# The values' projection of a fused encoder layer: one quarter of k goes from eight block products to seven

## The chip, the cores and the metric

The kernel runs on one core of one Trainium2 chip. The metric is the device time of one execution in microseconds (us), lower is better. The kernel before takes 1814.43 us (median of 3 runs, 1814.18 to 1815.42). Engines are called as the profile calls them: PE is TensorE (matmul), ACT is ScalarE, DVE is VectorE, POOL is GpSimd, SP is SyncE; SP and POOL here mainly issue DMAs. PSUM, where matmuls accumulate, has eight banks of 128 x 512 f32 on this kernel's count.

## The reference, cut to what matters

One layer of a streaming encoder on 256 tokens of width 2048. Of it, the change touches the input projection, and of that only the last 1024 columns, the values of the attention:

```python
h = rms_norm(x, mix_norm[i])
proj = h @ w_in[i]                  # (256 x 2048) @ (2048 x 4096)
u = proj[..., :SSM_WIDTH]           # 1024 columns; then q, k and v, 1024 each
v = proj[..., SSM_WIDTH + 2 * SB_WIDTH:].reshape(bsz, seq, SB_HEADS, SB_HEAD_DIM)
y_ssm = s5_mixer(u, ...)            # ends in a gate: z * sigmoid(z @ w_glu + b_glu)
y_sb = stick_breaking_attention(q, k, v.transpose(0, 2, 1, 3))
```

## The kernel before, in words

**Products in three parts.** All big products are taken in fp32r, in three parts: a weight piece of 256 rows by 512 columns (128 x 1024 in SBUF) is split into a rounded part `whi` (ACT, a CAST at line 182) and the rest `wlo` (DVE, a subtraction at line 185); the activations are split once into `nhi` and `nlo`. A product is hi x hi, hi x lo and lo x hi, summed in PSUM. Lines 341 and 346 are those matmuls in a plain block, lines 530, 531 and 533 in a group of seven (below). Each matmul is 128 x 128 against 128 x 512.

**A plain block** (`gemm_block`) takes 512 columns of a weight matrix. It goes over k in quarters of 512 rows (called kb 0 to 3; one DMA of 1 MB each, into a tile `raw`), each in two halves of 256 rows. A half is 12 matmuls: two token tiles of 128, times two k tiles of 128, times three parts. The two token tiles have a PSUM bank each (`acc`, four banks in turn). The values are two plain blocks before, so 2 x 8 x 12 = 192 matmuls, and `values` scales each bank into the tiles `v` on ACT (line 1554).

**A group of seven** (class `Seven`, used in the feed-forward parts) takes a quarter of k of two column blocks as a 2 x 2 problem: two token tiles and two k halves on the left, two k halves (b11, b21 of the first block, b12, b22 of the second) on the right. Instead of 8 products of 6 matmuls it needs 7, for which some operands are sums: of the weights, t1 = b11 + b12, t2 = t1 + b22, t4 = t2 + b21 (DVE, line 537, in `add`) and b12 + b22 (a DMA with accumulation, issued by POOL, line 598); of the activations, four sums made by `sum_forms` (DVE, line 487) and split into `hhi` and `hlo`. Every one of the seven right operands is split by ACT and DVE. In `single`, a form of it with few banks, products 1, 6 and 7 use one bank one after the other, and ACT or DVE takes the bank's contents out in between.

**What runs beside it.** Every half of a block ends in a call of `step()`, which hands one step to whatever was put off. During the values these are: the turning and scaling of the keys' second block (`qk_turn`, line 1327, and `qk_scale`, line 1334), the attention's scores for two pairs of heads (PE, lines 1354 to 1364), their logarithms and exponentials (ACT: Abs 1372, Exp 1373, Ln 1379, each change of function with an ACT_TABLE_LOAD), the splits `sph` and `spl` of the result, the sums over keys (PE, lines 1393 to 1400), and the splits `hhi` of the gate's input (`zt`). The gate's product (`glu`, lines 1489 to 1498) follows the values directly.

**What sets the order.** Each engine works its instructions off in the order in which they stand in its list; a scheduler of the framework sets these lists when the kernel is built, from its own estimate of when things are ready, and need not keep the program's order except where the code says `pin` or `issue_after`. Weights come through the tile `raw` of 1 MB, of which five exist; two hold x during the whole middle part, so three are in turn. Whatever is loaded next waits on SP for the release of the tile three loads back. Of `whi` and of `wlo` there are four each.

Of the kernel before, what the change touches and what calls it, by code (L numbers as in the profile page):

```python
# [12 lines left out]
AF = mybir.ActivationFunctionType  # L13
# [13 lines left out]
NB = 512  # L27
# [6 lines left out]
def layer_kernel(ctx: ExitStack, tc: tile.TileContext, a: dict, shapes: dict, out: bass.AP):  # L34
# [44 lines left out]
    def acc(s="acc"):  # L79
        return accp.tile([P, NB], F32, tag="acc", name=uid(s))  # L80
# [275 lines left out]
    def gemm_block(act, w, n0, nkt, first=()):  # L356

        ps = [acc(), acc()]
        for k0 in range(0, nkt, 4):
            part = act(k0 // 4)  # L360
            quarter = first[k0 // 4] if k0 // 4 < len(first) else weight_halves(w, k0, min(4, nkt - k0), n0)
            for half in list(quarter):
                k = k0 + 2 * half[0]
                gemm_half(ps, (part, half), range(TT), k == 0, k + 2 == nkt, in_turn=first and k0 == 0)
                if first and half[0] == 0 and k0 + 4 < nkt:
                    act(k0 // 4 + 1)
                step()
        return ps
# [123 lines left out]
    class Seven:  # L492
# [28 lines left out]
            self.last = split(hi, lo, src)  # L521
            return hi, lo

        def multiply(self, z, left, parts, final):
            hi, lo = parts
            ps = self.bank(z)
            begin = self.begin(z)
            lh, ll = left
            for j in range(2):
                nc.tensor.matmul(ps, lhsT=lh[j], rhs=hi[:, j], start=begin and j == 0, stop=False)  # L530
                nc.tensor.matmul(ps, lhsT=ll[j], rhs=hi[:, j], start=False, stop=False)  # L531
            for j in range(2):
                nc.tensor.matmul(ps, lhsT=lh[j], rhs=lo[:, j], start=False, stop=z in final and j == 1)  # L533

        def add(self, x, y):
            t = self.pool.tile([P, 2, NB], F32, tag="sum", name=uid("sum"), bufs=2)
# [22 lines left out]
        def single(self, kb, one, six, seven):  # L559
# [27 lines left out]
            put_off(0, nc.vector.tensor_tensor, seven, self.bank(7), six, ALU.add)  # L587
            step()

        def chunk(self, kb, final=()):  # L590

            if ring[0] is None:
# [956 lines left out]
    put_off(16, attn_out, pool, 0, ysb, sqa)  # L1549
    vt = [get(pool, f"v{t}") for t in range(TT)]  # L1550

    def values(n, ps):
        for t in range(TT):
            pin(nc.scalar.activation(vt[t][:, n * NB : (n + 1) * NB], ps[t], AF.Copy, scale=nm.rs(t)))
# [279 lines left out]
```

## Time and profile before

| | |
|---|---|
| median of 3 runs | 1814.43 us |
| the profiled execution, its own time | 1814.06 us |
| its span in the profile | 1812.3 us |
| PE busy | 1805.9 us, 8914 matmuls |
| DVE busy | 1573.8 us |
| ACT busy | 1063.8 us |
| granted clock of PE | 1.00 |
| the values' matmuls | from 853.8 to 903.3 us |

The span is what the profile covers, the execution's own time holds 1.8 us around it. "Busy" is the time in which an engine had something in work; a chain of waits follows, from the last instruction back, what each had to wait for. In the chain a matmul's piece goes from the end of the one before to its own end. A row of the timeline gives start, duration, engine, line, operation, `output<-inputs` with shapes, a count, and in brackets the idle time before it and what ended it.

### The profile page before, as it was taken

The numbers are of one execution on the slowest core, as the hardware profiler recorded it, in microseconds if no ns is written. First come the engines' busy times: TensorE is split into PE (matmuls) and PEld (weight loads), VectorE is DVE, ScalarE is ACT, GpSimd is POOL, SyncE is SP. The second block draws the span as 40 slices with busy tenths as digits, with TensorE's granted clock in tenths as the row PEclk, the third lists the DMA queues.
The fourth block names the chain that finished last, engine by engine and source line by source line (L and its number), as shares of the span: only waits on it lengthen the run. The fifth ranks groups of instructions, "written<-read, shape, count | busy, mean of one in ns | idle before, by whom it ended". The sixth has DMA issues, their size and how long they took to land.

```text
span 1812.3 us, 24211 instructions
## 1 busy us (share of the span) xinstructions
PE 1805.9 (100%) x8914; PEld 1497.3 (83%) x8914; DVE 1573.8 (87%) x1840; ACT 1063.8 (59%) x1240; POOL 104.8 (6%) x160
## 2 busy tenths in 40 slices
PE   9999999999999999999999999999999999999998
PEld 8888888888888888888898888888888888888887
DVE  7998889999998896697567899999999999889875
ACT  7445456555565665456695566555565556567664
POOL 0020100000000001010021000000000010000000
PEclk9999999999999999999999999999999999999999
DMA  9599867787776667674646687787767786666663
GB/s 382 208 306 309 253 220 234 238 276 219 256 274 209 197 229 257 190 256 156 219 147 219 226 300 221 265 269 233 233 232 240 239 273 229 239 209 224 200 244 128
DMA packets 107799, 428.41 MB, mean 236 GB/s; under 512 B 24512, under 2 KB 48352, under 8 KB 65280
## 3 DMA queue, kind: packets, MB, share of 16 engines
q1 hardware_dynamic: 96832, 391.15, 61.2%
q0 software_dynamic: 10560, 35.40, 9.0%
q8 instruction: 70, 1.15, 0.3%
q14 instruction: 49, 0.40, 0.1%
q10 hardware_dynamic: 288, 0.31, 0.1%
HBM read 372.41 MB, written 10.88 MB: 211 GB/s over the span
## 4 chain that ended last, share of the span: by engine, by line
PE 99%; DMA 1%; DVE 0%; ACT 0%; SPq 0%; issue 0%; DVEq 0%; ACTq 0%
PE acc L346 33%; PE acc L341 16%; PE aux L346 15%; PE aux L341 7%; PE acc L530 5%; PE acc L533 5%; PE acc L531 5%; PE aux L530 3%; PE aux L533 3%; PE aux L531 3%; DMA raw<-in_ffn_w_gate 1%; PE aux L1242 0%; PE acc L1498 0%; PE acc L1493 0%; PE acc L1489 0%; PE aux L1187 0%
## 5 line engine op out<-in xcount | busy, mean ns | idle before, releaser
L185 DVE TENSOR_TENSOR wlo<-raw,whi 128x1024 fp32r<-128x1024 f32 x478 | 579.4, 1225 | 124.0 <-ACT whi L182 117.4
L182 ACT CAST whi<-raw 128x1024 fp32r<-128x1024 f32 x478 | 496.3, 1050 | 291.9 <-PE acc L346 181.6
L346 PE MATMUL acc<-whi,nhi 128*128 128x512 f32 x908 | 355.7, 392 | 0.4 <-ACT whi L182 0.4
L346 PE MATMUL acc<-whi,nlo 128*128 128x512 f32 x908 | 353.3, 390 | 0.0
L341 PE MATMUL acc<-wlo,nhi 128*128 128x512 f32 x908 | 252.8, 389 | 0.0
L185 DVE TENSOR_TENSOR slo<-raw,shi 128x1024 fp32r<-128x1024 f32 x186 | 226.8, 1219 | 14.1 <-ACT shi L182 13.8
L182 ACT CAST shi<-raw 128x1024 fp32r<-128x1024 f32 x186 | 195.2, 1050 | 59.6 <-DMA raw<-in_ffn_w_down 23.5
L346 PEld LDWEIGHTS acc<-whi,nhi 128*128 128x128 f32 x908 | 170.6, 188 | 37.0 <-ACT whi L182 0.8
L341 PEld LDWEIGHTS acc<-wlo,nhi 128*128 128x128 f32 x908 | 170.5, 188 | 35.7 <-DVE wlo L185 0.3
L346 PEld LDWEIGHTS acc<-whi,nlo 128*128 128x128 f32 x908 | 170.8, 188 | 34.8
L182 ACT CAST whi<-sum 128x1024 fp32r<-128x1024 f32 x79 | 83.2, 1054 | 161.2 <-DVE sum L537 141.0
L182 ACT CAST shi<-sum 128x1024 fp32r<-128x1024 f32 x59 | 62.1, 1053 | 105.0 <-DVE sum L537 93.3
L537 DVE TENSOR_TENSOR sum<-sum,raw 128x1024 f32<-128x1024 f32 x92 | 112.5, 1222 | 0.9
L185 DVE TENSOR_TENSOR wlo<-sum,whi 128x1024 fp32r<-128x1024 f32 x79 | 96.5, 1224 | 5.2 <-ACT whi L182 4.5
L598 POOL DMA_DIRECT2D raw<-raw x44 | 38.1, 867 | 1032.6 <-DVE sum L537 722.4
L346 PE MATMUL aux<-whi,nhi 128*128 128x512 f32 x220 | 85.7, 390 | 0.0
L346 PE MATMUL aux<-whi,nlo 128*128 128x512 f32 x220 | 85.6, 389 | 0.0
L185 DVE TENSOR_TENSOR slo<-sum,shi 128x1024 fp32r<-128x1024 f32 x59 | 72.1, 1222 | 1.1 <-ACT shi L182 0.5
L341 PE MATMUL aux<-wlo,nhi 128*128 128x512 f32 x220 | 67.7, 389 | 0.0
L537 DVE TENSOR_TENSOR sum<-raw,raw 128x1024 f32<-128x1024 f32 x46 | 56.2, 1222 | 8.0 <-DMA raw<-in_ffn_w_down 7.2
L346 PE MATMUL acc<-whi,hhi 128*128 128x512 f32 x156 | 60.7, 389 | 0.0
L346 PE MATMUL acc<-whi,hlo 128*128 128x512 f32 x156 | 60.7, 389 | 0.0
(392 smaller groups left out, 3402.6 us busy)
## 6 DMA issues: line engine op xcount, KB each, us to landing
raw<-in_ffn_w_up SPq DMA_DIRECT2D x88, 1024.0 KB, 5.6
raw<-in_ffn_w_down SPq DMA_DIRECT2D x88, 1024.0 KB, 4.9
raw<-in_ffn_w_gate SPq DMA_DIRECT2D x86, 1024.0 KB, 7.1
raw<-in_w_in SPq DMA_DIRECT2D x32, 1024.0 KB, 5.3
raw<-raw POOLq DMA_DIRECT2D x46, 512.0 KB, 5.4
raw<-in_w_out SPq DMA_DIRECT2D x16, 1024.0 KB, 4.9
raw<-in_w_ple_gate SPq DMA_DIRECT2D x16, 1024.0 KB, 5.1
hT<-mid SPq DMA_DIRECT2D x160, 64.0 KB, 4.5
```

The costliest lines, as they stand in the source:

```text
L182: copy = nc.scalar.copy(hi, src)
L185: rest = nc.vector.tensor_tensor(out=lo, in0=src, in1=hi.bitcast(F32), op=ALU.subtract)
L341: nc.tensor.matmul(ps[t], lhsT=lh, rhs=lo[:, j, cols], start=False, stop=stop and j == 1)
L346: nc.tensor.matmul(ps[t], lhsT=(ahi, alo)[i][:, 2 * h + j, t * P : (t + 1) * P], rhs=hi[:, j, cols], start=start and j == 0 and i == 0, st ...
L530: nc.tensor.matmul(ps, lhsT=lh[j], rhs=hi[:, j], start=begin and j == 0, stop=False)
L531: nc.tensor.matmul(ps, lhsT=ll[j], rhs=hi[:, j], start=False, stop=False)
L533: nc.tensor.matmul(ps, lhsT=lh[j], rhs=lo[:, j], start=False, stop=z in final and j == 1)
L537: nc.vector.tensor_tensor(out=t, in0=x, in1=y, op=ALU.add)
L598: nc.gpsimd.dma_start(b12, b22, accum_op=ALU.add)
```

## The change

The two plain blocks of the values become one run over both blocks. First come kb 0, 1 and 2 of the first block in plain halves, then kb 3 of both blocks as one group of seven (`lean`, new), then kb 0, 1 and 2 of the second block in plain halves. The group uses four single `acc` banks: products 1, 6 and 7 add up in one (ACT copies the partial sums out after each, into what will be `v`), product 5 has one, and products 2 and 4 go straight into the first block's two banks. After the group those two are read out, and the second block's banks, with product 3 in one of them, come from the same pool. DVE puts the outputs together in `v` (`halfway`, `done`, `ended`), and ACT scales them there in place (`scaled`). The weight sums use the tile `h` (two of them) instead of tiles of their own; the sums of the activations for kb 3 are made after the first block's kb 1. `multiply` gets a flag for the builder's check of accumulation groups, and `chunk` a condition; neither does anything elsewhere.

```diff
+        def lean(self, kb, one, six, seven, halfway, done):
+            b11, b21, b12, b22 = self.load(kb)
+            whole, summed = self.lefts(kb)
+            t1 = self.add(b11, b12)
+            nc.gpsimd.dma_start(b12, b22, accum_op=ALU.add)
+            self.multiply(1, whole(0, 0), self.prepare(b11), shared, True)
+            self.product(5, summed(0), t1, shared)
+            step()
+            t2 = self.add(t1, b22)
+            self.product(2, whole(1, 0), b21, (2,))
+            parts = self.prepare(t2)
+            nc.scalar.copy(one, self.bank(1))
+            halfway(self)
+            self.banks[6] = self.banks[7] = self.bank(1)
+            self.begun |= {6, 7}
+            self.multiply(6, summed(1), parts, shared, True)
+            step()
+            t4 = self.add(t2, b21)
+            self.banks[3] = acc()
+            self.product(3, summed(3), b22, ())
+            parts = self.prepare(b12)
+            nc.scalar.copy(six, self.bank(1))
+            self.multiply(7, summed(2), parts, shared, True)
+            step()
+            parts = self.prepare(t4)
+            nc.scalar.copy(seven, self.bank(1))
+            self.multiply(4, whole(1, 1), parts, (4,))
+            done(self)
+            self.banks[8] = acc()
+            step()
...
-    def values(n, ps):
-        for t in range(TT):
-            pin(nc.scalar.activation(vt[t][:, n * NB : (n + 1) * NB], ps[t], AF.Copy, scale=nm.rs(t)))
-
-    for n in range(2):
-        put_off(2, values, n, gemm_block(nm, w_in, v0 + n * NB, KD))
+    def values():
+        even, odd = ([v[:, n * NB : (n + 1) * NB] for v in vt] for n in range(2))
+
+        def scaled(n):
+            for t in range(TT):
+                v = vt[t][:, n * NB : (n + 1) * NB]
+                pin(nc.scalar.activation(v, v, AF.Copy, scale=nm.rs(t)))
+
+        def halfway(s):
+            nc.vector.tensor_tensor(out=even[0], in0=s.bank(2), in1=even[0], op=ALU.add)
+
+        def done(s):
+            nc.vector.tensor_tensor(out=even[1], in0=s.bank(4), in1=odd[1], op=ALU.add)
+            for t in range(TT):
+                nc.vector.tensor_tensor(out=odd[t], in0=s.bank(5), in1=odd[t], op=ALU.subtract)
+            put_off(1, scaled, 0)
+
+        def ended(s):
+            for t, z in enumerate((3, 8)):
+                nc.vector.tensor_tensor(out=odd[t], in0=s.bank(z), in1=odd[t], op=ALU.add)
+            put_off(1, scaled, 1)
...
+        s = Seven(nm, forms.get, ((w_in, v0), (w_in, v0 + NB)), Rows(), None)
+        s.column(0, (0, 1))
+        forms[3] = sum_forms(s.pool, whole_rows(s.pool, nm(3)), "h")
+        s.column(0, (2,))
+        s.lean(3, even[0], *odd, halfway, done)
+        s.column(1, (0, 1, 2), True)
+        put_off(0, ended, s)
```

How the lists move is shown at three places. Outside of the values' stretch all five lists are the same but for the position of a few ACT and DVE instructions in the gate.

First, ACT at the start of kb 3. Before, the two CASTs of the first block's kb 3 are followed by the scaling of the keys (`k`, out of the bank pair in which they were turned) and by the CASTs of the second block's kb 0:

```order
L182 CAST whi_7717<-raw_7715 128x1024
L182 CAST whi_7721<-raw_7715 128x1024
L1334 ACTIVATE k_1383_7771<-aux_7706,gains 128x1024
L182 CAST whi_7777<-raw_7775 128x1024
L182 CAST whi_7781<-raw_7775 128x1024
L1372 ACTIVATE sp_7797<-aux_7741 128x768
```

Now (`raw_7726` holds b11 and b21, `raw_7728` holds b12 and b22, `h_7730`, `h_7766` and `h_7803` are t1, t2 and t4, `acc_7737` is the bank of products 1, 6 and 7):

```order
L182 CAST whi_7733<-raw_7726 128x1024
L606 COPY v_1355_7575<-acc_7737 128x512
L1370 ACTIVATE k_1400_7801<-aux_7717,gains 128x1024
L182 CAST whi_7744<-h_7730 128x1024
L182 CAST whi_7768<-raw_7726 128x1024
L182 CAST whi_7778<-h_7766 128x1024
L182 CAST whi_7806<-raw_7728 128x1024
L182 CAST whi_7816<-raw_7728 128x1024
L182 CAST whi_7830<-h_7803 128x1024
L616 COPY v_1355_7575<-acc_7737 128x512
L1408 ACTIVATE sp_7827<-aux_7759 128x768
L1409 ACT_TABLE_LOAD
```

The copy of product 1 and the keys' scaling stand between the CAST of b11 and that of t1, though the program asks for the copy only after the CAST of t2.

Second, ACT later in the values, from the last CAST ahead of the attention's Ln to the next CAST of a weight behind it. Before, four halves of the second block are cast by then (`raw_7775` and `raw_7815`):

```order
L182 CAST whi_7821<-raw_7815 128x1024
L1379 ACT_TABLE_LOAD
L1379 ACTIVATE sp_7797<-sp_7797 128x768
L1554 ACTIVATE v_1355_7575<-acc_7577,sm_6241 128x512
L1554 ACTIVATE v_1356_7576<-acc_7578,sm_6241 128x512
L182 CAST hhi_7853<-zt_7601 128x1024
L182 CAST sph_7857<-sp_7797 128x768
L1379 ACTIVATE sp_7812<-sp_7812 128x768
L182 CAST whi_7865<-raw_7863 128x1024
```

Now two halves of the second block are cast (`raw_7848`):

```order
L182 CAST whi_7854<-raw_7848 128x1024
L1409 ACTIVATE sp_7845<-sp_7845 128x768
L1415 ACT_TABLE_LOAD
L1415 ACTIVATE sp_7827<-sp_7827 128x768
L1594 ACTIVATE v_1355_7575<-v_1355_7575,sm_6241 128x512
L1594 ACTIVATE v_1356_7576<-v_1356_7576,sm_6241 128x512
L182 CAST hhi_7886<-zt_7601 128x1024
L182 CAST sph_7890<-sp_7827 128x768
L1415 ACTIVATE sp_7845<-sp_7845 128x768
L182 CAST whi_7898<-raw_7896 128x1024
```

The same run of work stands two CASTs nearer to the start of the second block, and has one Exp more in it.

Third, DVE in the group. Before there are only the subtractions of the plain halves at this place. Now:

```order
L185 TENSOR_TENSOR wlo_7734<-raw_7726,whi_7733 128x1024
L541 TENSOR_TENSOR h_7730<-raw_7726,raw_7728 128x1024
L541 TENSOR_TENSOR h_7766<-h_7730,raw_7728 128x1024
L185 TENSOR_TENSOR wlo_7745<-h_7730,whi_7744 128x1024
L185 TENSOR_TENSOR wlo_7769<-raw_7726,whi_7768 128x1024
L185 TENSOR_TENSOR wlo_7779<-h_7766,whi_7778 128x1024
L541 TENSOR_TENSOR h_7803<-h_7766,raw_7726 128x1024
L1597 TENSOR_TENSOR v_1355_7575<-acc_7587,v_1355_7575 128x512
L185 TENSOR_TENSOR wlo_7807<-raw_7728,whi_7806 128x1024
L185 TENSOR_TENSOR wlo_7817<-raw_7728,whi_7816 128x1024
L185 TENSOR_TENSOR wlo_7831<-h_7803,whi_7830 128x1024
```

The sum t4 (`h_7803`) stands behind the subtraction for t2. On PE the scores of the two pairs of heads stand within product 2 and behind product 6; on SP the loads of both blocks' kb 3 follow each other, where before eight small DMAs to `zt` stood between these two loads.

More of the change, by code (lines that the diff above doesn't have):

```diff
@@ L529, in multiply @@
             for j in range(2):
-                nc.tensor.matmul(ps, lhsT=lh[j], rhs=hi[:, j], start=begin and j == 0, stop=False)
-                nc.tensor.matmul(ps, lhsT=ll[j], rhs=hi[:, j], start=False, stop=False)
+                nc.tensor.matmul(
+                    ps, lhsT=lh[j], rhs=hi[:, j], start=begin and j == 0, stop=False, skip_group_check=joined
+                )
+                nc.tensor.matmul(ps, lhsT=ll[j], rhs=hi[:, j], start=False, stop=False, skip_group_check=joined)
             for j in range(2):
-                nc.tensor.matmul(ps, lhsT=lh[j], rhs=lo[:, j], start=False, stop=z in final and j == 1)
+                nc.tensor.matmul(
+                    ps, lhsT=lh[j], rhs=lo[:, j], start=False, stop=z in final and j == 1, skip_group_check=joined
+                )
         def add(self, x, y):
@@ L588, in single @@
             step()
+        def lean(self, kb, one, six, seven, halfway, done):
[28 more added lines that the diff above has]
+            step()
         def chunk(self, kb, final=()):
-            if ring[0] is None:
+            if ring[0] is None and self.turns:
                 ring[:] = [self.turns, 0]
@@ L1550, in layer_kernel, with tile @@
     vt = [get(pool, f"v{t}") for t in range(TT)]
[L1552 to L1557 removed]
+    def values():
[15 more added lines that the diff above has]
+            put_off(1, scaled, 1)
+        class Rows:
+            def tile(self, shape, dtype, tag, name, bufs):
+                return com("h").rearrange("p (j n) -> p j n", n=NB)
+        forms = {}
+        s = Seven(nm, forms.get, ((w_in, v0), (w_in, v0 + NB)), Rows(), None)
[5 more added lines that the diff above has]
+        put_off(0, ended, s)
+    values()
     put_off(12, attn_out, pool, 1, ysb, sqa)
```

2 lines of the change are left out of this document (1 added, 1 removed).

## The prediction

> **What bounds the kernel now.** I read the page's shares first, then PE's waits, then the stretch of the values. Here are the span, PE's busy time, the chain's shares by engine, and the whole answer on PE's waits:
>
> ```profile
> span 1812.3 us, 24211 instructions
> ...
> PE 1805.9 (100%) x8914; PEld 1497.3 (83%) x8914; DVE 1573.8 (87%) x1840; ACT 1063.8 (59%) x1240; POOL 104.8 (6%) x160
> ...
> PE 99%; DMA 1%; DVE 0%; ACT 0%; SPq 0%; issue 0%; DVEq 0%; ACTq 0%
> ```
> ```profile
> PE aux L252 <- POOL ones L125: 1.1, 1, 1.1
> PE acc L346 <- ACT whi L182: 0.4, 1, 0.4
> ```
>
> PE waits 1.5 us in all, near the start; from there to the end it is never without work. So a matmul taken away shortens the kernel by its spacing, and a wait put on PE anywhere lengthens it by its whole length, since no later idle time takes it back. The chain of waits gives PE's pace in the values (start, length, engine, tile, line, count; a piece runs from end to end):
>
> ```profile
> 870.98 1.83 PE acc L346 x8
> ...
> 873.72 0.24 PE aux L1354 x2
> ...
> 875.26 1.85 PE acc L346 x8
> ...
> 882.32 1.81 PE acc L346 x8
> 884.13 0.91 PE acc L341 x4
> 885.04 1.81 PE acc L346 x8
> ```
>
> A half of 12 matmuls takes 885.04 - 882.32 = 2.72 us, 0.227 each. kb 3 of the first block starts at 870.98, and one pair of heads' scores takes 875.26 - 873.72 = 1.54. Busy time by engine, for 860 to 910 and for its third stretch of 10 us:
>
> ```profile
> 880.00:890.00 10.00, 10.00 (x46) 8.26 (x45) 6.11 (x6) 9.97 (x13) 0.00 (x0) 1.00 0.37 136
> ...
> sum 50.00, PE 50.00 PEld 42.75 DVE 26.35 ACT 33.65 POOL 0.00; mean PE 10.00 PEld 8.55 DVE 5.27 ACT 6.73 POOL 0.00
> ```
>
> Over 50 us ACT has 16 to spare and DVE 24, but from 880 to 890 ACT has nothing (9.97 of 10). PE is not held up there only because four halves' CASTs were done ahead. That is the place to watch.
>
> **The change, part by part.** *Saved.* 42 matmuls stand for 48 in kb 3. Six at 0.227 are **1.36 us**, all that the change can win.
>
> *Added.* ACT gets the CAST of the summed activations, three CASTs more (seven operands, not four) and three copies out of PSUM. DVE gets eight full-size operations (three sums, three subtractions, one sum and one subtraction for the activations), four of a quarter and six of half that size, about 14 us at 1.18 each (the 2.36 for two in the next fence). The activations' sums fall into DVE's gap of 5.51 us and ACT's of 6.73 (its first row below) and cost nothing; without that gap they would come before the subtractions of the next half. The rest meets PE in the group, where the lists decide. ACT at kb 3, DVE at the same place, then ACT at an older group of the same kind (a copy of product 1 and the CAST behind it):
>
> ```profile
> 867.66 2.00 ACT L182 CAST whi<-raw 128x1024 fp32r<-128x1024 f32 x2 [6.73 <-DMA raw<-in_w_in]
> 871.02 1.11 ACT L1334 ACTIVATE k<-aux,gains 128x1024 f32<-128x1024 f32 x1 [1.36 <-PE aux L1327]
> ```
> ```profile
> 868.74 2.36 DVE L185 TENSOR_TENSOR wlo<-raw,whi 128x1024 fp32r<-128x1024 f32 x2 [5.51 <-ACT whi L182]
> ```
> ```profile
> 139.30 0.58 ACT L572 COPY sg<-acc 128x512 f32<-128x512 f32 x1
> 139.77 1.06 ACT L182 CAST whi<-raw 128x1024 fp32r<-128x1024 f32 x1
> ```
>
> *The first wait: the copy of product 1 ahead of the CAST of t1.* ACT's list now reads CAST of b11, copy, keys' scaling, CAST of t1. The copy needs product 1 finished: 870.98 + 6 x 0.227 = 872.34. ACT, done with b11 by about 868.7, stands still until then, and queued behind it are the scaling and all CASTs of the group. From 872.34: 0.04 to begin (the scaling began 0.04 after its matmuls, 871.02), 0.47 for the copy (139.77 - 139.30), 1.11 less 0.09 for the scaling (neighbours on ACT overlap about 0.1), 1.05 for the CAST: 874.92. PE's next matmuls, product 5, need just that CAST, and PE works in order: it waits 2.58. A restart costs more than the gap; the one restart of the trace, as the chain has it:
>
> ```profile
> 16.03 1.06 ACT whi L182
> 17.09 0.04 issue
> 17.13 0.96 PE acc L346 x3
> ```
>
> Three matmuls end 1.00 after the CAST instead of 0.68, so 0.32 on top: **2.90 us**. Before, nothing stood there: the second half's CAST followed the first at once. From below: t1 is there earlier than ACT can use it (next part), so the order on ACT alone sets this, and only the single steps can be off, by some 0.3 in all.
>
> *Loads and the accumulating DMA.* SP now issues both loads of kb 3 back to back, at about 862, past eight small DMAs. Two such loads, 0.5 apart, and the older accumulating DMAs landed so (us from issue):
>
> ```profile
> DMA to landing us min/median/max: 4.9/5.9/6.8
> ```
> ```profile
> DMA to landing us min/median/max: 4.5/5.3/8.6
> ```
>
> The second of the pair (6.8) would land at 869.4; DVE makes t1 behind the subtraction of b11, by 871.1, 2.9 us before ACT reaches it. POOL's DMA, which waits for t1 and has nothing else queued, then lands at 876.5, at worst 879.8. ACT reaches the CAST of b12 at 877.8. CAST and copy behind it are not due before 879.6 (t4, below), so the median costs nothing and the worst 0.9. The delayed `zt` DMAs land long before their use near 891.
>
> *The second wait: ACT's long run with half the lead.* After the first wait PE does products 5, 2 and 6 and one pair's scores: 874.92 + 0.32 + 18 x 0.227 + 1.54 = 880.87 at the end of product 6. DVE's t4 (three subtractions ahead of it, four operations at 1.18) is there at 879.7 and its CAST at 880.7, just in time, so that product 6 sets the next copy. From there ACT has this work, timed before:
>
> ```profile
> 875.30 0.81 ACT L1372 ACTIVATE sp<-aux 128x768 f32<-128x768 f32 x1
> 876.13 1.28 ACT L1373 ACT_TABLE_LOAD   x1
> 877.42 0.85 ACT L1373 ACTIVATE sp<-sp 128x768 f32<-128x768 f32 x1
> 879.60 0.81 ACT L1372 ACTIVATE sp<-aux 128x768 f32<-128x768 f32 x1 [1.33 <-PE aux L1364]
> 880.30 1.04 ACT L182 CAST whi<-raw 128x1024 fp32r<-128x1024 f32 x1
> 881.24 0.85 ACT L1373 ACTIVATE sp<-sp 128x768 f32<-128x768 f32 x1
> 881.99 1.04 ACT L182 CAST whi<-raw 128x1024 fp32r<-128x1024 f32 x1
> 883.04 1.28 ACT L1379 ACT_TABLE_LOAD   x1
> 884.34 0.85 ACT L1379 ACTIVATE sp<-sp 128x768 f32<-128x768 f32 x1
> 885.09 1.25 ACT L1554 ACTIVATE v<-acc,sm 128x512 f32<-128x512 f32 x2
> ...
> 888.64 1.99 ACT L182 CAST whi<-raw 128x1024 fp32r<-128x1024 f32 x2
> ```
>
> By starts: 0.04, copy 0.47, Abs 0.83, table 1.29, Exp 0.75 (881.99 - 881.24), CAST 0.95, copy 0.47, Abs 0.70, CAST 0.95, Exp 0.85, and then the run from the table load to the end of the next CAST, 883.04 to 889.64, 6.60: together 13.90, to 894.77. PE has work for scores 1.54, products 3, 7 and 4 (4.09) and the two halves already cast (5.44): 11.07, to 891.94. Before, four halves were cast ahead of that run and PE never saw it. Now it waits 2.83, with the restart **3.15 us**. The two scalings in the run read `v`, not PSUM; no row has that at this size, and I take the 1.25 for two that the old ones took; a CAST of twice the size from SBUF takes 1.04, so 0.2 less is the other end.
>
> *No third wait.* Behind this ACT has five CASTs in a row and finds PE still in its third half of the block; the loads of the gate come some 4 us later and PE with them. DVE's outputs sit in stretches that ACT leaves it, and the banks they release are wanted later.
>
> **Sum:** -1.36 + 2.90 + 3.15 = **+4.7 us**. The profiled execution took 1814.06, the median 1814.43, 0.4 apart; against the median 1819.1. Steps off by 0.3 in either chain and the DMA's 0.9 give 1818.2 to 1820.6 for this case.
>
> **The rivals.** *Only one wait.* The second is a difference of 2.83 between chains of 13.90 and 11.07, either of which can be off by a position: if ACT reaches the copy behind product 6 or the CASTs of the second block some 3 us sooner relative to PE, or PE is held a little in the group by DVE, the second wait merges into the first. Then +2.90 - 1.36, 1816.0. For it speaks that ACT's steps overlap more when queued; against it that every item of the run is in the list.
>
> *Not slower: the copies come free.* If the blocked time of ACT is only what it would have waited anyway, PE gets its CASTs in time, and 1.36 us is kept: 1813.1. It decides at the CAST of t1: the price turns from none to a loss once that CAST ends after 872.34. For it: ACT has 16 us to spare around here. Against it: the copy's place ahead of the CAST, which leaves no path under 2.5.
>
> *The clock drops after a wait.* The start shows PE cold (128 x 128 matmuls, then pairs of the usual kind):
>
> ```profile
> 1.14 3.78 PE L252 MATMUL aux<-ones 128*128 128x128 f32 x16 [1.14 <-POOL ones L125]
> 4.80 1.19 PE L346 MATMUL acc<-whi,nhi 128*128 128x512 f32 x2
> ...
> 6.60 0.63 PE L341 MATMUL acc<-wlo,nhi 128*128 128x512 f32 x2
> ```
>
> Four matmuls take 6.60 - 4.80 = 1.80 there, 0.45 each, twice 0.227. Slow from 1.14 to 6.60, 5.5 us, of which half is lost: 2.7 per drop, 1821.8. In the kernel before no gap is long enough to try it (the longest after the start is 0.4); the two predicted are 2.6 and 2.9. The Trainium skill (TensorE: Matmul & The Clock Gate, "What's actually happening") puts the fall to half rate after an idle window of about 3.4 us that runs free; no run here shows that. By that rule gaps of 2.6 and 2.9 keep the clock, and one stretched past 3.4 by a late DMA could lose it.
>
> **How the numbers follow.** Both waits 0.60, one wait 0.22, free copies 0.06, a drop of the clock 0.12. The likeliest gives 1819.1. Beyond 0.2% (3.6 us, about what a measurement of this kernel can tell) slower means above 1818.1: nearly all of the first case (0.54) and the last (0.12), 0.66. Within 0.2%: one wait, free copies and the rest, 0.31. Faster by more needs 3.6 us where 1.36 can be had: 0.03. The range takes in one wait and reaches into the drop: 1815.7 to 1821.5.
>
> **What would show it.** In the profile after, PE's waits list two for ACT: one of 2.6 at product 5 for a `whi` made from `h`, one of about 2.9 at the second block's kb 1 for a `whi` from `raw`; ACT's copy of product 1 has idle time before it, ended by PE; the gate's first matmul comes at 908 instead of 903.28; the granted clock stays 1.00. Wrong: no wait at product 5 (then the copy did not hold ACT), a wait there ended by DVE or a load (then t1 is late), or a wait elsewhere of over 1 us.

## The result, and the profile after

The changed kernel takes 1821.47 us (median of 6 executions, 1820.55 to 1823.93), the kernel before 1814.45 beside it (1813.91 to 1815.42). The ratio is 1.0040, with a 95% interval of 1.0029 to 1.0050: slower by 7.0 us where 4.7 was forecast. The median lies at the very end of the predicted range (1821.5), and above the 1818.2 to 1820.6 that were given for the likeliest case. The profiled execution took 1821.41.

First the shares of the page and the whole answer on PE's waits, after the change:

```profile
span 1819.6 us, 24227 instructions
...
PE 1807.5 (99%) x8908; PEld 1498.0 (82%) x8908; DVE 1588.4 (87%) x1858; ACT 1069.5 (59%) x1247; POOL 104.3 (6%) x161
...
PE 96%; DMA 1%; ACT 1%; DVE 1%; SPq 0%; issue 0%; ACTq 0%; POOLq 0%; DVEq 0%
```
```profile
PE acc L346 <- ACT whi L182: 3.4, 2, 3.1
PE acc L530 <- ACT whi L182: 2.7, 1, 2.7
PE aux L252 <- POOL ones L125: 1.1, 1, 1.1
```

PE does six matmuls fewer and is nevertheless 1.6 us longer busy; and the chain of waits is on PE for 96% of the span, where it was 99%. There are two new waits, both for ACT. On PE's timeline after (start, duration; in brackets the idle time before), they stand between the turning of the keys and the gate's first matmul, and so does one thing more:

```profile
869.61 1.03 PE L1363 MATMUL aux<-ident,sg 128*128 128x128 f32 x8
...
874.69 0.50 PE L530 MATMUL acc<-whi,hhi 128*128 128x512 f32 x1 [2.67 <-ACT whi L182]
...
894.87 0.79 PE L346 MATMUL acc<-whi,nhi 128*128 128x512 f32 x1 [3.08 <-ACT whi L182]
895.47 0.63 PE L346 MATMUL acc<-whi,nlo 128*128 128x512 f32 x1
895.89 0.63 PE L346 MATMUL acc<-whi,nhi 128*128 128x512 f32 x1
...
902.33 0.39 PE L346 MATMUL acc<-whi,nhi 128*128 128x512 f32 x1
902.55 0.40 PE L346 MATMUL acc<-whi,nlo 128*128 128x512 f32 x1
...
910.60 0.28 PE L1525 MATMUL acc<-hhi,whi 128*128 128x256 f32 x1
```

The same two ends in the kernel before:

```profile
869.95 1.03 PE L1327 MATMUL aux<-ident,sg 128*128 128x128 f32 x8
...
903.11 0.28 PE L1489 MATMUL acc<-hhi,whi 128*128 128x256 f32 x1
```

From the first to the last of these it was 33.16 us, and is 40.99: the whole loss, 7.83, lies in this stretch (it begins 0.34 sooner, so the gate starts 7.5 later). It holds 161 matmuls before and 155 after, the same ones but for the six saved. I use this stretch below as a local measure; it leaves out the scatter of the rest of the span. After the second wait the matmuls come 0.42 us apart (895.89 - 895.47) instead of 0.22 (902.55 - 902.33). Windows of 3.41 us after the change, laid so that their edges fall on the changes of clock (columns: window, length, busy us and instructions of PE, of PEld, of DVE, ACT and POOL, granted clock of PE, DMA share, GB/s):

```profile
870.12:873.53 3.41, 1.90 (x11) 1.31 (x9) 2.45 (x2) 1.43 (x2) 0.92 (x1) 1.00 0.38 93
873.53:876.94 3.41, 2.25 (x11) 1.81 (x12) 2.27 (x2) 3.41 (x5) 0.00 (x0) 1.00 1.02 315
890.58:893.99 3.41, 1.21 (x6) 0.67 (x4) 2.21 (x3) 3.41 (x6) 0.00 (x0) 1.00 0.67 274
893.99:897.40 3.41, 2.53 (x6) 2.05 (x7) 3.41 (x4) 3.41 (x5) 0.00 (x0) 0.50 0.00 0
897.40:900.81 3.41, 3.41 (x9) 2.64 (x9) 3.41 (x5) 2.89 (x4) 0.00 (x0) 0.50 0.62 197
900.81:904.22 3.41, 3.41 (x18) 2.85 (x18) 2.42 (x4) 1.05 (x1) 0.00 (x0) 1.00 0.59 192
```

The granted clock fell to half at 893.99, while PE was still waiting, and came back at 900.81. PE worked 2.53 + 3.41 us of that at half rate, which costs half of it, some 3.0 by this estimate. With the waits: -1.36 + 2.67 + 3.08 + two restarts of 0.3 + 3.0 = 8.0, against 7.83. (A restart is what PE loses behind a wait beside its length, since its first matmuls come slower.) So the loss has three parts, and the third, the clock, is the one that the forecast left out.

What ACT did, in its timeline after, in the order that the lists show:

```profile
872.10 0.59 ACT L606 COPY v<-acc 128x512 f32<-128x512 f32 x1 [4.39 <-PE acc L535]
872.58 1.12 ACT L1370 ACTIVATE k<-aux,gains 128x1024 f32<-128x1024 f32 x1
873.59 1.04 ACT L182 CAST whi<-h 128x1024 fp32r<-128x1024 f32 x1
...
880.83 0.58 ACT L616 COPY v<-acc 128x512 f32<-128x512 f32 x1
...
890.15 1.32 ACT L1594 ACTIVATE v<-v,sm 128x512 f32<-128x512 f32 x2
...
893.79 1.98 ACT L182 CAST whi<-raw 128x1024 fp32r<-128x1024 f32 x2
```

ACT stood still for 4.39 us ahead of the copy of product 1, and the CAST of t1 behind it ended at 874.63, where PE starts. The run from the copy of product 6 to the CAST that PE waits for took from 880.83 to 894.8. The chain of waits after the change, in order of time, shows from where ACT came there:

```profile
862.35 8.12 DMA raw<-in_w_in
...
870.49 1.24 DVE h L541
...
871.76 0.55 issue
...
872.32 6.51 DMA raw<-raw
...
878.93 0.44 ACT whi L182
```

The second of the two loads issued back to back took 8.12 us, the accumulating DMA 6.51 and 0.55 until its issue. ACT began the CAST of b12 at 878.93, a little over a microsecond later than foreseen; that filled the slack that it had there and no more, since the copy of product 6 began at 880.83 against the forecast of 880.91. Whether the DMA alone held that CAST is not shown by this trace: a matmul of product 2 ended 0.01 us after the DMA landed, and ACT's own timeline names that one. The run with the copy held back, below, tells them apart.

### The profile page after: what moved, and what is told of

It reads as the page before. It is cut to its first block, busy times and chain, and to the rows that moved or that the text cites. A ratio compares the mean times of both kernels' runs of the same rounds, so it can differ in the third digit from the quotient of the medians.

```text
span 1819.6 us, 24227 instructions
## 1 busy us (share of the span) xinstructions
PE 1807.5 (99%) x8908; PEld 1498.0 (82%) x8908; DVE 1588.4 (87%) x1858; ACT 1069.5 (59%) x1247; POOL 104.3 (6%) x161
## 3 DMA queue, kind: packets, MB, share of 16 engines
q8 instruction: 70, 1.15, 0.3%
## 4 chain that ended last, share of the span: by engine, by line
PE 96%; DMA 1%; ACT 1%; DVE 1%; SPq 0%; issue 0%; ACTq 0%; POOLq 0%; DVEq 0%
PE acc L346 31%; PE acc L341 16%; PE aux L346 15%; PE aux L341 7%; PE acc L530 5%; PE acc L535 5%; PE acc L533 5%; PE aux L535 3%; PE aux L533 3%; PE aux L530 3%; DMA raw<-in_ffn_w_gate 1%; DMA raw<-in_w_in 0%; PE aux L1278 0%; PE acc L1534 0%; PE acc L1529 0%; PE acc L1525 0%
## 5 line engine op out<-in xcount | busy, mean ns | idle before, releaser
L346 PE MATMUL acc<-whi,nhi 128*128 128x512 f32 x892 | 350.6, 394 | 3.5 <-ACT whi L182 3.4
L346 PE MATMUL acc<-whi,nlo 128*128 128x512 f32 x892 | 348.1, 391 | 0.0
L346 PE MATMUL acc<-whi,hhi 128*128 128x512 f32 x156 | 60.7, 389 | 0.0
L530 PE MATMUL acc<-whi,hhi 128*128 128x512 f32 x146 | 57.3, 392 | 2.7 <-ACT whi L182 2.7
```

Source lines behind the costliest of these rows:

```text
L346: nc.tensor.matmul(ps[t], lhsT=(ahi, alo)[i][:, 2 * h + j, t * P : (t + 1) * P], rhs=hi[:, j, cols], start=start and j == 0 and i == 0, st ...
```

## The experiments

Every run was timed beside the kernel before on its own chip (medians of before: 1813.03 us for the first four runs below; 1813.18 for the changed kernel run again, for both waits filled and for the first two orders without waits; 1813.24 for the rest), so times are given as a difference from that. A fall is a drop of the granted clock to 0.50. Executions of one kernel differ by whether the clock fell in them, and by more than executions without a fall differ among themselves. So I list the executions one by one, sorted.

My theory when I started: the loss is the two waits, ordered by ACT's list, and the clock that falls in the second. The rivals were that the waits are tied to one another through the accumulating DMA, so that neither can be mended alone, and that the clock falls for a reason other than idle time.

### The scalings of v moved out of ACT's run

```diff
-            put_off(1, scaled, 0)
+            put_off(5, scaled, 0)
```

> The two scalings of v (1.23 us together) that stand on ACT ahead of the CAST for the second block's kb 1 are put off by four steps; the list then has that CAST behind hhi, ahead of sph and Ln. By its starts in the changed kernel (hhi at 891.38, then sph 0.74, Ln 0.74, two CASTs) the CAST's first half ends at about 892.1 instead of 894.8. Theory (the second wait is ACT's run, and the fall of the clock hangs on the length of that wait): the wait at product kb 1 goes from 3.08 to 0.3 or 0.4 us, the clock stays at 1.00 in every slice, the time is 1821.5 - 2.7 - 2.75 = 1816.0 (the first wait of 2.67 stays). Rival (the clock falls for another reason, say the group's load as such or the first wait): the wait shrinks but the clock still falls, 1818.8. Rival (the wait is not set by what stands ahead of the CAST, but by a load or by DVE): 1821.5 or at most 1.2 less.

Measured: median 1817.34, ratio 1.0021 (1.0012 to 1.0030). Executions: before + 2.6, 2.7, 2.8, 3.2, and + 4.0, 4.3, 4.5, 4.6, 4.7, 4.8, 4.9. PE's waits, the first of them on its timeline, and its windows around that, in this run:

```profile
PE acc L530 <- ACT whi L182: 2.7, 1, 2.7
...
PE acc L346 <- ACT whi L182: 0.5, 2, 0.3
PE acc L341 <- DVE wlo L185: 0.2, 1, 0.2
```
```profile
873.89 0.50 PE L530 MATMUL acc<-whi,hhi 128*128 128x512 f32 x1 [2.67 <-ACT whi L182]
```
```profile
871.47:874.88 3.41, 0.99 (x4) 0.71 (x5) 1.85 (x2) 3.41 (x5) 0.92 (x1) 1.00 0.93 309
874.88:878.29 3.41, 3.41 (x11) 2.86 (x11) 3.41 (x4) 1.81 (x3) 0.00 (x0) 0.50 0.77 157
878.29:881.70 3.41, 3.41 (x19) 2.94 (x19) 1.77 (x3) 2.26 (x3) 0.00 (x0) 1.00 0.65 202
```

The second wait went from 3.08 to 0.3, as expected: it is ACT's run, and two items of that run decide it. But the clock did not stay. Here it fell at the first wait, the same 2.67 us that had kept it in the changed kernel; it fell at 874.88, a microsecond after PE had started again, and stayed low for one window of 3.41 us, half of which, 1.7, is lost. The sum without a fall is -1.36 + 2.67 + 0.5 + 0.2 and restarts, some 2.5 to 2.9: four executions lie there, and seven 1.7 or so above. So a wait of 2.67 can cost the clock too, and whether it does changes from one execution to the next. My expectation of 1816.0, before + 1.55, had taken it as safe, and left out restarts and the 0.2 for DVE.

### The copy of product 1 held back

```diff
-            nc.scalar.copy(one, self.bank(1))
+            with tc.issue_after(self.last[0]):
+                nc.scalar.copy(one, self.bank(1))
```

> The copy of product 1 is held back behind the CAST and the subtraction of t2, so ACT's list reads CASTs of b11, t1, b21, t2, then copy and the keys' scaling. Theory: the first wait falls from 2.67 to about 0.8 us (t1 itself is there only at 871.7, since the second load of the pair lands late, and its CAST ends at 872.8), but the accumulating DMA still lands at 878.8 and with it the CAST of b12 and all of ACT's long run keep their places, so the second wait grows by what the first gave up, to about 5 us, with the clock falling: 1821.5, no gain. Rival (the two waits are independent, the second moves with PE): 1821.5 - 1.9 = 1819.6. Rival (the first wait alone makes the loss): 1821.5 - 2.9 = 1818.6 or less.

Measured: median 1820.52, ratio 1.0041 (1.0028 to 1.0054), + 7.1, 7.2, 7.5, 7.7, 8.2. PE's waits, and the place on ACT where the gain went:

```profile
PE acc L346 <- ACT whi L182: 4.1, 1, 4.1
PE acc L530 <- ACT whi L182: 1.2, 1, 1.2
```
```profile
878.53 1.05 ACT L182 CAST whi<-raw 128x1024 fp32r<-128x1024 f32 x1 [1.68 <-DMA raw<-raw]
```

The first wait lost 1.5 us and the second won 1.0; 1.9 had been expected for each, so both moved the way foreseen but less far. ACT now stands for 1.68 us, and here it is the accumulating DMA that ends it; all of its long run keeps its place. The time is that of the changed kernel: mending the first wait alone brings nothing. By their times all five executions had a fall (the waits alone make -1.36 + 1.2 + 4.1 + 0.6 = 4.5): wherever the windows of 3.41 us lie, one of them holds at least half of the 4.1, 2.05.

### The same, and the sum b12 + b22 on DVE

```diff
-            nc.gpsimd.dma_start(b12, b22, accum_op=ALU.add)
+            nc.vector.tensor_tensor(out=b12, in0=b12, in1=b22, op=ALU.add)
```

> As the run before, and the sum b12 + b22 is made on DVE (one more full-size operation, 1.2 us) instead of by the accumulating DMA. Theory: the first wait is about 0.8, and now ACT's run is free of the DMA's landing and starts with product 6, 1.9 us earlier, so the second wait is about 3 us again: 1819.6 if the clock falls in it as in the changed kernel, 1816.9 if it does not. If the landing of the DMA had no part in the second wait, this run and the one before give the same time.

Measured: median 1818.20, ratio 1.0031 (1.0020 to 1.0042), + 4.4, 4.5, 4.9, 5.2, and + 6.3, 6.7, 7.3. PE's waits:

```profile
PE acc L346 <- ACT whi L182: 3.8, 2, 2.6
...
PE acc L530 <- ACT whi L182: 0.8, 1, 0.8
```

Expected were 1819.6 and 1816.9, that is before + 5.2 with and + 2.5 without a fall. Both kinds are there, each some 2 us later: a wait of 1.15 (3.8 - 2.65) with its restart, which I had not foreseen, stands at the second block's kb 0, and the first wait keeps its restart too. The median is 2.3 below the run before, so the landing of the DMA did have its part once the first wait was shorter. The waits together gave up only some 0.5 of that (5.3 to 4.8); the rest goes with the clock, which four of these seven executions kept by their times.

### PE kept busy in the second wait, and in both

All-zero matmuls into open banks (their all-zero input is made once, at the start); here the first place with 11 and the second with 13. The filled kernels of this section and the next differ in these two counts alone.

```diff
+            for i in range(11):
+                pin(nc.tensor.matmul(
+                    self.bank((2, 4)[i % 2]), lhsT=ident_r, rhs=none_r.unsqueeze(1).to_broadcast([P, 4, P]), start=False,
+                    stop=False, skip_group_check=True,
+                ))
             self.product(5, summed(0), t1, shared)
...
-        s.column(1, (0, 1, 2), True)
+        s.column(1, (0,))
+        for i in range(13):
+            pin(nc.tensor.matmul(
+                s.bank((3, 8)[i % 2]), lhsT=ident_r, rhs=none_r.unsqueeze(1).to_broadcast([P, 4, P]), start=False,
+                stop=False, skip_group_check=True,
+            ))
+        s.column(1, (1, 2), True)
```

The second place alone:

> The changed kernel with 13 more matmuls (right side all zero, added into the two open banks, so nothing changes in the sums) between the second block's kb 0 and kb 1, that is in the 3.08 us in which PE has nothing. 13 x 0.227 = 2.95 us. The CAST that PE waits for is where it was. Theory (the wait costs its length and, apart from that, the idle time in it makes the clock fall, 2.75 us): with PE busy the clock stays at 1.00, the gate starts some 3 us earlier though PE does 13 matmuls more, the time is 1821.5 - 2.75 - 0.3 (no restart) = 1818.5. Rival (the clock falls because of something else at that place): the time is 1821.5 or, with the matmuls slowed, more.

Measured: median 1819.96, ratio 1.0037 (1.0024 to 1.0049), + 5.5, 6.0, and + 6.9, 7.1, 8.3. After the run with the scalings this reads easily: the second wait is filled, the first (2.67) is still there, and by their times it takes the clock in three executions of five. The profiled one kept it throughout and took 1818.57, before + 5.5. Expected was before + 4.1 (1818.5 beside 1814.45): the 0.2 and 0.5 left of the second wait, and the restarts, were not in that sum (-1.36 + 2.67 + 2.95 + 0.7 + 0.6 makes 5.6). This run alone can't show whether the fall in the second wait went with the idle time, since the first wait makes falls of its own; the next pair does.

Then the changed kernel itself again, and both places filled, on one chip:

> The changed kernel itself once more, beside the others on one chip. The waits are the same in every execution (2.67 and 3.08); without a fall of the clock they make before + 5.0 (-1.36 + 2.67 + 3.08 + two restarts of 0.3). Theory (the clock falls where some 2 us of a free-running stretch of 3.41 us are idle, and stays low for one or two stretches, 1.7 or 3.4 us lost): the times fall into steps, before + 5.0, + 6.7 and + 8.4, mostly the middle one, with granted clocks of 0.999 to 0.996. Rival (a steady cost that I have not found): all executions within 0.5 us of before + 7.0.

> The changed kernel with 11 all-zero matmuls ahead of product 5 and 13 ahead of the second block's kb 1, so that PE has work in both waits; ACT, DVE and the loads keep their order. 24 x 0.227 = 5.4 us of work for PE, some 0.2 of each wait left, 0.5 for a subtraction that DVE has late behind the second. Theory (the fall of the clock belongs to the idle time): before + 5.3 in every execution, spread under 1 us, clock 1.00 at 870 to 905: some 1.7 us less than the changed kernel though PE does 24 matmuls more. Rival (the clock falls for other reasons, or the loss is not the clock): before + 7 or more, with the same spread as the changed kernel.

Measured for the changed kernel: median 1820.84, ratio 1.0039 (1.0026 to 1.0051), + 5.1, 5.3, and + 7.7, 7.8, 9.1. With both filled: median 1818.89, ratio 1.0031 (1.0020 to 1.0043), + 5.3, 5.5, 5.7, 5.8, 5.8, 6.1. The profiled execution of the changed kernel happened to be one of the two without a fall; its PE waits, and the two ends of the stretch in it:

```profile
PE acc L346 <- ACT whi L182: 3.7, 2, 3.4
PE acc L530 <- ACT whi L182: 2.7, 1, 2.7
```
```profile
868.90 1.03 PE L1363 MATMUL aux<-ident,sg 128*128 128x128 f32 x8
...
907.39 0.28 PE L1525 MATMUL acc<-hhi,whi 128*128 128x256 f32 x1
```

This pair settles the clock. The waits alone, 2.67 and 3.40 here, with restarts and the six matmuls saved, make -1.36 + 6.07 + 0.6 = 5.3, and that is what the two executions without a fall show; the forecast of + 4.7 was this kernel without a fall. The stretch says the same: it takes 38.49 us here, 5.33 more than before. It is 2.50 shorter than in the execution shown first, although its second wait is 0.32 longer, so the fall cost 2.8 us there. With 24 matmuls more, in the same time that PE would have idled, no execution has a fall by its time, the spread is 0.8 instead of 4 us, and the median is 2 us lower than that of the changed kernel. The intervals of the two ratios overlap; it is the two kinds of execution in the one and the single kind in the other that tell them apart. The rival of a steady cost is out: the changed kernel's own executions lie 4 us apart. The mean granted clocks agree: 0.997 and 0.998 for the three slower executions of the changed kernel, 0.999 and 1.000 for the other two, and with both places filled 1.000 in five and 0.999 in one. In the profiled execution with both places filled the granted clock was 1.00 from 870 to 880 and from 890 to 900.

### How long an idle time takes the clock

The first place filled in all three, the second with none, 4 and 6 matmuls.

> The changed kernel with the 11 all-zero matmuls in the first wait only; the second stays open, 3.1 to 3.4 us. Without a fall the time is the one with both filled, before + 5.5 or so (a wait and the work that fills it take the same time). Theory (free-running stretches of 3.41 us; the clock falls at the end of one in which more than some 2 us were idle; so a gap of 3.2 is caught at about (3.41 + 3.2 - 3.9) / 3.41 = 0.8 of the positions): about 4 of 5 executions at + 7.2 or + 8.9, the others at + 5.5. Rival (the first wait, not the second, makes the clock fall): + 5.5 in all.

> The same with 4 matmuls, which leaves about 2.3 us. Theory (threshold near 2 us, between the 1.5 of a stretch that kept the clock and the 2.2 of one that lost it): the clock falls in about half of the executions, (3.41 + 2.3 - 3.9) / 3.41 = 0.5, so times at + 5.6 and + 7.3. Rival (a whole idle stretch of 3.4 us is needed): + 5.6 in all.

> Both waits filled as before, but the second with 6 matmuls of 13, which leaves a gap of about 1.8 us. Theory (some 2 us of idle time in one stretch are needed): the clock never falls, before + 5.6 in every execution with a spread under 1 us. Rival (any gap of this kind may do it, or the threshold is at half a stretch, 1.7 us): some executions at + 7.3.

Measured, with the gap of the profiled execution: none (3.00 us): median 1819.49, ratio 1.0037 (1.0023 to 1.0051), + 5.7, 5.8, 6.2, 6.8, 8.4. Four (2.24): median 1819.86, ratio 1.0034 (1.0021 to 1.0046), + 4.5, 5.8, and + 6.6, 6.7, 7.4. Six (1.64): median 1818.46, ratio 1.0029 (1.0018 to 1.0041), + 4.9, 5.0, 5.2, 5.2, 5.3, and one at + 6.8. The profiled execution with four had a fall; its windows around it:

```profile
891.17:894.58 3.41, 1.24 (x6) 0.69 (x4) 2.36 (x3) 3.41 (x6) 0.00 (x0) 1.00 0.48 202
894.58:897.99 3.41, 3.34 (x8) 2.66 (x9) 3.41 (x4) 3.41 (x5) 0.00 (x0) 0.50 0.00 0
897.99:901.40 3.41, 3.41 (x17) 2.78 (x16) 3.41 (x4) 2.09 (x3) 0.00 (x0) 1.00 0.86 303
```

The 2.24 us were enough; a wholly idle window of 3.41 is not needed, so that rival is out. In the windows that ended in a fall PE was idle for 2.17 (3.41 - 1.24) here, 2.20 in the changed kernel, 2.42 in the first experiment and 2.65 in the third; only with the copy held back was one idle throughout.

Why a gap of 3.40 kept the clock while one of 2.24 lost it can be read from the same traces. Each ends with one more fall, behind the last matmul. In the changed kernel that one is at 1819.00, 925.01 us after the one at 893.99, which is 271 times 3.4133; in the other four executions with a fall the distance is 921.60 (three times) or 938.67, 270 and 275 times 3.4133. So the windows stand in a fixed grid through an execution, and the last fall tells where they lay in executions that had no other. The first fence has the two windows around the 3.40 of the changed kernel run again, and its last fall at 1814.38, 270 times 3.4133 behind their common edge. Then come the last fall of the changed kernel, and a window at the end of the order with the DMA (next section):

```profile
889.36:892.78 3.42, 1.70 (x8) 1.08 (x6) 1.72 (x2) 3.42 (x6) 0.00 (x0) 1.00 0.91 307
892.78:896.19 3.41, 1.74 (x8) 1.43 (x9) 3.41 (x5) 3.41 (x5) 0.00 (x0) 1.00 0.00 0
1814.38:1816.50 2.12, 0.00 (x0) 0.00 (x0) 0.00 (x0) 0.00 (x0) 0.00 (x0) 0.50 0.11 39
```
```profile
1819.00:1819.60 0.60, 0.00 (x0) 0.00 (x0) 0.00 (x0) 0.00 (x0) 0.00 (x0) 0.50 0.00 0
```
```profile
1804.72:1808.13 3.41, 1.59 (x6) 0.64 (x4) 2.68 (x4) 0.90 (x2) 0.00 (x0) 1.00 0.51 186
```

The edge cut the 3.40 into 1.72 (3.42 - 1.70) and 1.67, and neither part took the clock. Laid out like this, all windows behind the start of all 14 profiled executions of this record fall into two groups, without an exception: where PE was idle for 1.82 us or less (the last row, 3.41 - 1.59) the clock stayed at 1.00, where it was idle for 2.17 or more the clock fell at the window's end. So the bound lies between 1.82 and 2.17, and whether a gap costs the clock is decided by where the grid cuts it. If the grid may lie anywhere, the 2.67 of the first experiment is caught in a share of (3.41 + 2.67 - 2 x 2.17) / 3.41 = 0.5 to 0.7 of the executions, and 7 of 11 were; for the 3.00 it is 0.6 to 0.8, and three of five look like it; for the 2.24 it is 0.4 to 0.6, and three of five were. The counts agree with my rule, but so few executions can't test it closely. The 1.64 agrees but for one execution of six that I can't explain and that has no profile (the kernel before had one at + 1.4 and one at + 2.0 in 16 beside it).

### The order without waits

The waits taken away by order alone. The first of the three kernels against the change, cut to its steps:

```diff
-            nc.gpsimd.dma_start(b12, b22, accum_op=ALU.add)
...
-            self.product(5, summed(0), t1, shared)
+            self.product(2, whole(1, 0), b21, (2,))
             step()
+            self.product(5, summed(0), t1, shared)
+            with tc.issue_after(self.last[0]):
+                nc.scalar.copy(one, self.bank(1))
             t2 = self.add(t1, b22)
-            self.product(2, whole(1, 0), b21, (2,))
             parts = self.prepare(t2)
-            nc.scalar.copy(one, self.bank(1))
...
             self.product(3, summed(3), b22, ())
+            nc.vector.tensor_tensor(out=b12, in0=b12, in1=b22, op=ALU.add)
             parts = self.prepare(b12)
...
-            for steps, stage in ((0, scores), (2, exps), (4, logs), (5, parts), (7, passes), (9, weights)):
+            turns = (0, 3, 6, 7, 8, 9) if hp < 2 else (0, 2, 4, 5, 7, 9)
+            for steps, stage in zip(turns, (scores, exps, logs, parts, passes, weights)):
...
-    put_off(11, glu_in, zs, 0)
-    put_off(13, glu_in, zs, 1)
+    put_off(12, glu_in, zs, 0)
+    put_off(14, glu_in, zs, 1)
...
-            put_off(1, scaled, 0)
+            put_off(5, scaled, 0)
```

> Both waits are taken away by order and not by filling: product 2 goes ahead of product 5; the copy of product 1 stands behind the CAST of t1; the sum b12 + b22 is made on DVE, after t4; the scalings of v come four steps later, the gate's splits one step later, and for the two pairs of heads the Abs and Exp one step later, the Ln and their splits two, their sums over keys one. ACT's list then has both CASTs for kb 0 ahead of the copy of product 7, and both for kb 1 ahead of the Ln. Theory (the loss is nothing but where ACT's work stands): no wait of over 0.5 us left in the values, clock 1.00, and the six saved matmuls show: before - 1.0 (from - 1.36 to + 0.3). Rival (the group as such costs more than it saves, through DVE or the loads): a new wait for DVE or a load, before + 1 or more.

The same with the accumulating DMA (its line back in its place, the DVE sum out):

> As the run before, but the sum b12 + b22 stays with the accumulating DMA, as in the change. It lands at about 878.8, the CAST of b12 ends at about 879.9, and product 7 is due at about 880.8 behind product 3. Theory (its landing decided in the changed kernel only because ACT's long run stood behind it): the same time as the run before, within 0.5 us. Rival (the landing holds ACT up in any order): 1 to 2 us more than the run before, with a wait at product 7 or at the second block's kb 0.

And the DVE sum ahead of t4 instead of ahead of the CAST of b12:

> The order without waits, with one more step: the sum b12 + b22 stands on DVE ahead of t4 instead of behind it. In the run before it was ready at 879.2, the CAST of b12 ended at 880.3 and product 7's matmul spacing there was 0.71 instead of 0.23; now the sum is ready at about 877, the CAST ends at 879 and product 7 finds it. The other short hold, 0.69 at the second block's kb 1, stays (two Exp stand ahead of its CAST). Theory (each short hold costs its gap and a restart, some 0.35 together): before - 1.0. Rival (the holds are not what keeps the run before from the 1.36): before - 0.7 as in the run before.

Measured: with the sum behind t4, median 1812.41, ratio 0.9996 (0.9987 to 1.0005); with the DMA 1812.96, 0.9999 (0.9991 to 1.0008); with the sum ahead of t4 1812.29, 0.9994 (0.9985 to 1.0003), so - 0.8, - 0.2 and - 0.95 us against the kernel before. The intervals hold no change in all three; of the last one's 11 executions, nine lie below the lowest of 16 of the kernel before (1812.81). PE's waits with the DMA, and the two ends of the stretch in the last:

```profile
...
PE acc L530 <- ACT v L617: 0.7, 1, 0.7
```
```profile
868.99 1.03 PE L1364 MATMUL aux<-ident,sg 128*128 128x128 f32 x8
...
900.77 0.28 PE L1527 MATMUL acc<-hhi,whi 128*128 128x256 f32 x1
```

The stretch of the last takes 31.78 us, 1.38 less than before: the six matmuls' 1.36, all of it. So in this order the group costs PE nothing; the loss was in the order of the lists, ACT's above all. The DMA still costs something: 0.7 at product 7, which waits for ACT's copy of product 6 behind the CAST of b12, and 0.6 in the stretch more than the DVE sum behind t4 (33.15 against 32.56). The two medians, 0.55 apart, can't tell theory from rival in that test; the wait at product 7 is the rival's, with half its price. And the sum ahead of t4 freed the hold at product 7, as expected; the other, at kb 1, was gone too (PE was busy for all 31.78 us).

## Why the prediction was right or wrong

*The six matmuls, 1.36:* right, shown by the last order (1.38).

*The first wait, 2.58:* right. It is at product 5, for a `whi` made from `h`, and is 2.67; ACT's copy has its idle time ended by PE.

*The second wait, 2.83:* right in place and cause, 3.08 in size (3.00 to 3.40 in other executions). Taking two scalings out of the run ahead of the CAST took it to 0.3.

*The restarts, 0.32 each:* right. The stretch of the execution without a fall leaves 0.3 for each (5.33 + 1.36 - 6.07 = 0.62).

*The loads and the DMA:* the load pair's second took 1.3 longer than assumed (8.12 for 6.8), the DMA 1.2 longer (6.51 for 5.3), with 0.55 to issue it. "The median costs nothing" held with the slack used up; that the late landing ties the second wait to the first, so that mending the first alone brings nothing, was not in the text and is what the held-back copy showed.

*The step that failed:* the sum took PE's clock as 1.00 through both waits, and so put the price of half rate at nothing. "The clock drops after a wait" stood only as a rival with 0.12, because gaps of 2.6 and 2.9 were said to "keep the clock". The runs showed a granted clock of 0.50 from 893.99 to 900.81, which cost 2.8 us; the terms that the sum did have come to -1.36 + 2.67 + 3.08 + 0.6 = 5.0, close to its 4.7. Filling both waits with 24 matmuls ended the falls and took 2 us off the median, so the idle time is their cause. By their times at least four of the first six executions of the changed kernel had a fall (1.6 us or more above 1814.45 + 5.3; the other two are 0.8 and 0.9 above it), and three of five on the other chip.

The Trainium skill (TensorE: Matmul & The Clock Gate, "What's actually happening") says that the window runs free, and the fixed grid of windows of 3.41 us here agrees; what I read into it is that the whole window has to be idle, and the measurement decides against that: 2.17 of 3.41 idle were enough.

I also put too much on a rule that no run had shown, when two gaps of unknown effect stood in the sum. The likeliest case should have carried a drop, and 1819.1 + 2.7 is 1821.8, the rival's own figure. That this comes so close to 1821.47 is in part luck: the 2.7 is half of a cold start of 5.5 us, and the fall in the profiled execution came to 2.8 because it lasted two windows; a fall of one costs 1.7. And the range holds the median only because its upper end was drawn toward this rival.

*Its own test:* the gate's first matmul was to come 4.7 later with a clock of 1.00; it came 7.5 later, with a clock of 0.50 on the way, and so the trace alone names the missing term.

*The rivals:* one wait merging into the other was wrong (both are there); the free copies were wrong for this order, but the 1.36 can be had with the copies on ACT, so their place ahead of the CASTs was the reason, as argued. *No third wait:* right.

## What to carry to other kernels

Price a new wait on TensorE in two parts, its length and the clock: here a gap cost another 1.7 to 2.8 us of half rate behind it whenever some 2.2 us of it fell into one window of 3.41 us. Where the windows lie changes from execution to execution, so one profiled execution tells only one of the outcomes. A kernel whose TensorE never stops has no slack anywhere to take a wait back, so a saving of six matmuls is lost by a single instruction that stands in the wrong place on another engine; look in that engine's list for instructions that wait for TensorE ahead of ones that TensorE waits for. And mend all waits of a chain at once before judging a change: here the first mended alone gave nothing, as a DMA held the second in its place, and the second mended alone gave less than half of the loss.

## What the runs showed of the hardware that was not expected

The granted clock fell to 0.50 after gaps of 2.24, 2.65, 2.67, 3.08 and 4.10 us, and kept 1.00 over gaps of 1.64, 2.67, 3.00 and 3.40 in other profiled executions. What decided was the idle time within one window of a fixed grid of 3.4133 us: 1.82 us or less kept the clock, 2.17 or more lost it, at the window's end. So it could fall up to 1 us after PE had started again (874.88, PE busy from 873.89 in the first experiment). It came back after one window where PE was busy in nearly all of that window (idle for 0.07 us or less), and after two, 6.82 us, where the first still held 0.88 us of the wait. The second of two loads of 1 MB issued back to back took 8.12 us, where the pair shown of before had taken 4.9 and 6.8.
